# First norm of a two-block layer: its factors moved behind the transposes, a small first transfer, products of zeros at the start, and rstd sums on the vector engine

## Chip, cores and metric

The kernel runs on one core of a Trainium2 chip. The metric is the device time of one execution in microseconds (us), as the median of the timed runs. Five engines work side by side: PE (TensorE: products and transposes), DVE (VectorE), ACT (ScalarE), POOL (GpSimd) and SP (SyncE), which here issues the transfers from memory (DMA). Each engine takes its instructions in its own fixed order.

## The reference, cut to what matters

x is 256 tokens of width 1024, all float32. A first block adds a mixer of three branches and a feed-forward with a short convolution; a second block of two layers follows, then a last norm. Every part begins with a norm. Only the beginning matters here:

```python
def rmsnorm(x, g):
    y = x * lax.rsqrt(jnp.mean(x * x, axis=-1, keepdims=True) + EPS)
    return y * g

def first_block(x, ...):
    h = rmsnorm(x, norm_mix_g)
    c_q, c_kv, k_r, u_ssm, x_q, gate_logits = split_combined(h @ w_in)
    y_a = mla_branch(c_q, c_kv, k_r, ...) @ w_o_mla      # latent attention, rotated
    y_b = s5_branch(u_ssm, ...) @ w_o_ssm                # state space
    y_c = cross_branch(x_q, mem, ...) @ w_o_cross        # attention to mem, its norm first
    x = x + (g0 * y_a + g1 * y_b + g2 * y_c) @ w_out     # g0, g1, g2 = sigmoid(gate_logits)
    ...
```

## The kernel before

**Tiles.** The 256 tokens are two tiles of 128, with the tokens on the partitions. Before a product the normed rows are transposed by PE, so that the width lies on the partitions: eight blocks of 128 rows, four to a bank. Every float32 operand of a product is split into a rounded high part and the rest: for weights `wh` on ACT and `wl` on DVE (`raw` is the transfer's tile, 512 KB each), for normed rows `h` on both. Three products (high-high, high-low, low-high) stand for one. PE is thus the engine with the most work by design.

**The first norm** (`norm_T`, L551, and `norm_rows`, L533): per token tile, ACT squares two halves of 512 columns and sums them (`ss`), DVE multiplies by the gain (`xs`), POOL adds the two sums and EPS and takes the power -0.5 (`rs`), DVE scales `xs` by it, PE transposes (`tr`), ACT and DVE split the bank into `h`. The gain is loaded twice 128 x 512, one row to all partitions (`load_gain`). The first product of `w_in` (`pr`, 512 wide, 48 products for both token tiles) gives the query latents `cq` and a part of `ckv`.

**The state-space branch** (`ssm_setup`, `ssm_maps`, `ssm_half`): from small parameters in the tile `par`, ACT takes a sine and a cosine (`psin`, `pcos`), POOL forms powers of the factors (`pwr`) and from them the input factors `bwr`; DVE multiplies them into maps (`pm`, `xB`, `cT`, `x`), PE transposes those (`tr<-par,xB`) and forms `se`; POOL makes the angles' tables `turn`; DVE turns the inputs (`sp`), scans (`sv`) and turns back (`sg`); PE multiplies by `cT` (`yb<-sg,cT`). This runs in two halves. The second half's `yb` must be there before the glu and the last branch can be done. Meanwhile PE fills its time with gate products (`pt`, 256 wide, from `proj_T`).

**What sets the order.** All instructions are recorded with an estimated cost (`Program.add`, `Engine.cost`) and then issued by a list schedule (`forward`, `issue`): on each engine the ready instruction with the earliest latest-start goes next, within the limits of the tile pools (65 slots `w`, 5 `raw`, 8 banks). Transfers of kind "first" go ahead of all others. Any change of a cost, an operand or an engine can therefore move instructions far away, up to the end of the mixer; behind it the order is nearly the same.

[...]

Of the kernel before, what the change touches and what calls it, by code (L numbers as in the profile page):

```python
# [9 lines left out]
F32 = mybir.dt.float32  # L10
F32R = mybir.dt.float32r
# [31 lines left out]
def region(ap):  # L43
    """The partitions and the elements of a row that an access path may touch."""
    (row, parts), *free = ap.ap
    p, f = divmod(ap.offset, row)
    lo = f + sum(min(0, s * (n - 1)) for s, n in free)
    hi = f + sum(max(0, s * (n - 1)) for s, n in free) + 1
    return p, p + parts, lo, hi
# [10 lines left out]
class Op:  # L60
    """An instruction to come: its engine, its call and its estimated time."""
# [7 lines left out]
class Program:  # L69
    """Records instructions with their data's order and issues them by a list schedule.  # L70

    Per engine, the instruction that is ready and comes first by priority goes next, as long
    as the rest of the program can still run in the order of an earlier schedule within the
    tile pools. The priorities are start times of the schedule that runs from the end.
    """

    ENGINES = ("pe", "act", "dve", "pool", "sp")
    # time from the end of an instruction to the start of one on another engine that waits for it
# [19 lines left out]
    def tile(self, t, tags, whole=False):  # L98
        """Makes a tile known: the pools it takes room in, and if any two accesses keep their order."""
        name = t.tensor.name  # L100
        self.tags[name] = tags
        if whole:
            self.whole.add(name)
        return t

    def add(self, eng, call, cost, reads, writes, kind=""):
        op = Op(eng, call, cost, kind)
        # the vector engine's second port to SBUF is Pool's only one
# [35 lines left out]
    def backward(self, order):  # L144
        """Latest start times, from a schedule that runs from the end, later instructions of order first."""
# [42 lines left out]
    def forward(self, prio, base):  # L188
        """A schedule by priority; base is an order that keeps within the pools."""
# [32 lines left out]
        def room(i, full):  # L222
            """The tiles that op i takes into use, or None when there is no room for them."""
# [126 lines left out]
class Engine:  # L350
    """An engine's calls, recorded with their cost."""
# [33 lines left out]
class Ctx:  # L385
    """Pools, constants, and the blocks shared by all layers."""
# [43 lines left out]
    def weights(self, w, n0, n):  # L430
        """w[:, n0:n0+n] as the two float32r parts of a product, per 128-row block a list of (hi, lo)."""
# [34 lines left out]
    def mm3(self, ps, x, w, start, stop):  # L466
        """ps (+)= x.T @ w, the small product of the low parts left to float32's rounding."""
# [4 lines left out]
    def mm_rows(self, ps, xs, ws, start, stop):  # L472
        """ps[i] (+)= sum over k of xs[k].T @ ws[i][k], the products with the low parts of x last."""
# [16 lines left out]
    def rstd(self, ss, n, count):  # L490
        m = self.sm("rs_m", n)
        self.pool.tensor_scalar(out=m, in0=ss, scalar1=1.0 / count, scalar2=EPS, op0=ALU.mult, op1=ALU.add)
# [3 lines left out]

    def split(self, src, hi, lo, scale=None):
        """Splits float32 data into two float32r parts, scaled by a constant or per partition."""
# [14 lines left out]
    def transposes(self, src, name="tr"):  # L513
        """[128, 128 n] to a bank with the n blocks transposed."""
# [11 lines left out]
    def load_gain(self, src, kind="load"):  # L526
        """A gain vector of 1024, on all partitions."""
# [5 lines left out]
    def norm_rows(self, halves, g):  # L533
        """rmsnorm of [128, 1024] rows given as two halves."""
        ss = self.sm("ss", 2)
        xs = [self.w("xs") for _ in range(2)]
        for b in range(2):
            junk = self.w("junk")
            # D is an even power of two: the scale is exact
            self.act.activation(out=junk, in_=halves[b], func=AF.Square, scale=D ** -0.5, accum_out=ss[:, b:b + 1])  # L540
            self.dve.tensor_tensor(out=xs[b], in0=halves[b], in1=g[b], op=ALU.mult)
        s1, r = self.sm("s1", 1), self.sm("rs", 1)
        self.pool.tensor_scalar(out=s1, in0=ss[:, 0:1], scalar1=EPS, scalar2=None, op0=ALU.add)
        self.pool.tensor_tensor(out=s1, in0=s1, in1=ss[:, 1:2], op=ALU.add)
        self.pool.tensor_tensor(out=r, in0=s1, in1=self.mhalf[:, :1], op=ALU.pow)
# [4 lines left out]
    def norm_T(self, tiles, g):  # L550
        """rmsnorm of 256 rows, transposed and split: per half of the width (hi, lo), each [128, 2, 4, 128]."""  # L551
# [9 lines left out]

    def split_tokens(self, ps, dst, t):
        """Splits [128, 4 * 128] into the columns of token tile t of dst."""
# [3 lines left out]
    def norm_x(self, gain):  # L567
        """The norm of both token tiles of x, for the products to come."""
# [10 lines left out]
    def proj(self, w, n0, n, x=None, rows=False):  # L579
        """x.T @ w[:, n0:n0+n], per token tile; with rows one tile after the other."""  # L580
# [19 lines left out]
    def proj_T(self, w, n0, x=None):  # L600
        """w[:, n0:n0+256].T @ x for all tokens: two blocks of 128 rows in a bank."""
# [14 lines left out]
    def merge_out(self, m, scale, w):  # L616
        """x += (scale * m).T @ w, m as four tiles of two 128-row blocks of all tokens."""
# [16 lines left out]
    def swiglu(self, w1, w3, w2):  # L634
        """x += 0.5 * (silu(h w1) * (h w3)) w2."""
# [22 lines left out]
    def conv_swiglu(self, w_up, w_down, cw, cb):  # L658
        """x += (silu(g) * v) w_down with [g | v] the causal convolution of h w_up along the tokens."""
# [39 lines left out]
    def feed_forward(self, w1, w3, w2, gate_rows, gate, scale):  # L699
        """x += scale * gate(h w1, h w3) w2, by chunks of the inner width.  # L700

        The first chunk takes the token tiles one after the other, as the norm hands them over."""
# [43 lines left out]
    def gate_proj(self, w, n0, bias=None):  # L746
        """Gate of one branch, two blocks of 128 rows to a tile; with half the bias, tanh of half the logits."""
# [839 lines left out]
```

## Time and profile before

| | us |
|---|---|
| median of 3 runs (lowest to highest) | 1621.19 (1621.08 to 1621.62) |
| span of the profiled execution, first to last instruction | 1619.3 |
| PE busy in the span | 1589.3 (98%) |
| DVE, ACT, POOL busy | 1019.0, 843.1, 134.9 |

The profiled execution's own time is known by its span only; the median of the timed runs is 1.9 us longer, for what lies around the span. An engine's busy time counts from an instruction's start to its end, so the instructions of one engine may overlap a little. PE's own waits are few and lie nearly all in the first 220 us.

### The profile page before, as it was taken

What the parts mean: (1) busy time and instruction counts of PE and PEld (TensorE: products, weight loads), DVE (VectorE), ACT (ScalarE), POOL (GpSimd) and SP (SyncE); (2) the same over time, 40 slices, a digit from 0 to 9 for tenths busy, and PEclk for the clock granted to TensorE, in tenths of its full rate; (3) what the DMA queues carried; (4) which work ended last, traced back from release to release, by engine and by line L of the source; (5) the groups of instructions that cost most, each with busy time, mean ns of one, the idle gap of its engine ahead of it and who ended that gap; (6) DMA issues with size and microseconds to landing.
All of it is one profiled execution on the core that took longest, in us unless ns stands there. A gap on an engine that the chain in (4) does not pass through costs nothing.

```text
span 1619.3 us, 28502 instructions
## 1 busy us (share of the span) xinstructions
PE 1589.3 (98%) x11126; PEld 1455.3 (90%) x11126; DVE 1019.0 (63%) x1759; ACT 843.1 (52%) x1746; POOL 134.9 (8%) x276
## 2 busy tenths in 40 slices
PE   7999999999999999999999999999999999999998
PEld 6889989899989999889998999899998899989997
DVE  6678797787676545755657554665457556574543
ACT  6984554665555434555446443454345554464431
POOL 4554500000000000000000000000000000000000
PEclk9999999999999999999999999999999999999999
DMA  8731464665557575454647666475654546475650
GB/s 258 232 104 53 148 208 130 221 202 176 184 171 248 170 228 183 145 181 137 195 138 234 195 197 193 142 243 169 224 182 146 180 137 196 137 236 194 197 181 26
DMA packets 214374, 288.30 MB, mean 178 GB/s; under 512 B 13792, under 2 KB 170080, under 8 KB 214240
## 3 DMA queue, kind: packets, MB, share of 16 engines
q1 hardware_dynamic: 214240, 286.49, 55.6%
q8 instruction: 87, 1.43, 0.4%
q14 instruction: 47, 0.39, 0.1%
HBM read 284.88 MB, written 1.05 MB: 177 GB/s over the span
## 4 chain that ended last, share of the span: by engine, by line
PE 91%; DVE 4%; ACT 2%; DMA 2%; issue 1%; POOL 0%; SPq 0%; POOLq 0%; DVEq 0%; ACTq 0%
PE pt L463 50%; PE acc L463 22%; PE pr L463 7%; PE up L463 7%; PE tr L488 2%; DVE wl L379 1%; ACT wh L379 1%; PE yb L463 1%; DMA x<-in_x_dram 0%; DVE sbp L379 0%; DVE pm L379 0%; PE rs L463 0%; DMA raw<-in_w_mem_kv_dram 0%; PE glu L463 0%; ACT sqh L379 0%
## 5 line engine op out<-in xcount | busy, mean ns | idle before, releaser
L379 DVE TENSOR_TENSOR wl<-raw,wh 128x512 fp32r<-128x512 f32 x1045 | 661.3, 685 | 210.3 <-ACT wh L379 189.5
L463 PE MATMUL pt<-h,wh 128*128 128x256 f32 x4224 | 758.4, 282 | 0.1
L379 ACT CAST wh<-raw 128x512 fp32r<-128x512 f32 x1045 | 580.5, 618 | 158.4 <-DMA raw<-in_w_in_dram 48.1
L463 PEld LDWEIGHTS pt<-h,wh 128*128 128x128 f32 x4224 | 650.3, 188 | 3.4 <-ACT gate L379 0.3
L463 PE MATMUL pt<-h,wl 128*128 128x256 f32 x2112 | 593.2, 281 | 0.0
L463 PEld LDWEIGHTS pt<-h,wl 128*128 128x128 f32 x2112 | 397.7, 188 | 0.2 <-issue 0.2
L463 PE MATMUL acc<-wh,gh 128*128 128x512 f32 x440 | 173.7, 395 | 0.0
L463 PE MATMUL acc<-wh,gl 128*128 128x512 f32 x440 | 173.2, 394 | 0.0
L463 PE MATMUL acc<-wl,gh 128*128 128x512 f32 x440 | 173.2, 394 | 0.0
L463 PE MATMUL pr<-wh,h 128*128 128x512 f32 (+2 forms) x480 | 134.6, 362 | 2.1 <-ACT h L379 1.5
L379 ACT CAST gh<-sg 128x512 fp32r<-128x512 f32 x47 | 29.1, 620 | 151.5 <-DVE sg L379 151.5
L463 PE MATMUL up<-wh,h 128*128 128x512 f32 x320 | 102.0, 397 | 0.0
L463 PEld LDWEIGHTS pr<-wh,h 128*128 128x128 f32 x480 | 85.5, 189 | 17.2 <-ACT h L379 1.9
L463 PEld LDWEIGHTS acc<-wh,gl 128*128 128x128 f32 x440 | 82.6, 188 | 19.5
L463 PEld LDWEIGHTS acc<-wl,gh 128*128 128x128 f32 x440 | 82.6, 188 | 18.1
L463 PEld LDWEIGHTS acc<-wh,gh 128*128 128x128 f32 x440 | 82.6, 188 | 18.0
L379 POOL TENSOR_SCALAR s<-ss 128x1 f32<-128x1 f32 x20 | 9.9, 494 | 1059.1 <-ACT junk L379 1059.0
L379 DVE TENSOR_TENSOR sg<-sg,pt 128x512 f32<-128x512 f32 x36 | 24.7, 687 | 114.9 <-PE pt L463 114.9
L379 ACT ACTIVATE sg<-pt 128x512 f32<-128x512 f32 x36 | 21.6, 599 | 135.3 <-PE pt L463 135.3
L463 PE MATMUL pr<-wl,h 128*128 128x512 f32 (+2 forms) x240 | 86.5, 361 | 0.5 <-DVE wl L379 0.5
L463 PEld LDWEIGHTS up<-wh,h 128*128 128x128 f32 x320 | 59.7, 188 | 13.8
L379 ACT ACTIVATE junk<-x 128x512 f32<-128x512 f32 x36 | 22.8, 632 | 87.1 <-DVE x L379 80.9
(346 smaller groups left out, 1665.0 us busy)
## 6 DMA issues: line engine op xcount, KB each, us to landing
raw<-in_w_ffn_dram SPq DMA_DIRECT2D x264, 512.0 KB, 5.0
raw<-in_w_in_dram SPq DMA_DIRECT2D x124, 512.0 KB, 4.9
raw<-in_w_up_dram SPq DMA_DIRECT2D x44, 512.0 KB, 4.9
raw<-in_w_out_dram SPq DMA_DIRECT2D x24, 512.0 KB, 4.1
raw<-in_w_down_dram SPq DMA_DIRECT2D x22, 512.0 KB, 4.4
raw<-in_w_mem_kv_dram SPq DMA_DIRECT2D x8, 512.0 KB, 5.2
raw<-in_w_branch_ret_dram SPq DMA_DIRECT2D x8, 512.0 KB, 3.8
raw<-in_w_o_mla_dram SPq DMA_DIRECT2D x4, 512.0 KB, 4.7
```

Source lines behind the costliest of these rows:

```text
L379: self.prog.add(self.name, lambda: getattr(self.eng, op)(**kw), self.cost(op, kw), list(aps.values()), writes, "fast" if self.name == "dve ...
L463: self.prog.add("pe", lambda: self.nc.tensor.matmul(ps, lhsT=lhsT, rhs=rhs, start=start, stop=stop), ns, [lhsT, rhs], [ps])
L488: self.prog.add("pe", lambda: self.nc.tensor.transpose(out, src, ident), 109, [src, ident], [out])
```

## The change

The first norm alone gets a function of its own, `first_norm`. One square over 1024 columns gives the sum; `xs` is x times rstd, with no gain; after the transposes the width lies on the partitions, so the gain is a column of eight numbers per partition, and the split of each 128-column block takes it as its scale: sixteen small splits on ACT and DVE each instead of four wide ones. The gain and the identity for the transposes form a new tile `par0` (136 columns), loaded behind the first token tile; the other parameters (`par1`, 118 columns) are an ordinary load. `warm_up` adds eleven products of a zeroed tile, 512 columns wide in bfloat16, ahead of all other work of PE; nothing reads their bank. In all norms the sum with EPS moves from POOL to DVE (`row_rstd`, `rstd`), the power stays on POOL. The diff also drops comments and docstrings (left out here).

```diff
     def rstd(self, ss, n, count):
         m = self.sm("rs_m", n)
-        self.pool.tensor_scalar(out=m, in0=ss, scalar1=1.0 / count, scalar2=EPS, op0=ALU.mult, op1=ALU.add)
+        self.dve.tensor_scalar(out=m, in0=ss, scalar1=1.0 / count, scalar2=EPS, op0=ALU.mult, op1=ALU.add)
...
+    def row_rstd(self, ss):
+        s1, r = self.sm("s1", 1), self.sm("rs", 1)
+        if size(ss) == 1:
+            self.dve.tensor_scalar(out=s1, in0=ss, scalar1=EPS, scalar2=None, op0=ALU.add)
+        else:
+            self.dve.tensor_scalar(out=s1, in0=ss[:, 0:1], scalar1=ss[:, 1:2], scalar2=EPS, op0=ALU.add, op1=ALU.add)
+        self.pool.tensor_tensor(out=r, in0=s1, in1=self.mhalf[:, :1], op=ALU.pow)
+        return r
...
     def norm_rows(self, halves, g):
...
-        s1, r = self.sm("s1", 1), self.sm("rs", 1)
-        self.pool.tensor_scalar(out=s1, in0=ss[:, 0:1], scalar1=EPS, scalar2=None, op0=ALU.add)
-        self.pool.tensor_tensor(out=s1, in0=s1, in1=ss[:, 1:2], op=ALU.add)
-        self.pool.tensor_tensor(out=r, in0=s1, in1=self.mhalf[:, :1], op=ALU.pow)
+        r = self.row_rstd(ss)
...
+    def first_norm(self, gcol):
+        out = []
+        for b in range(2):
+            pair = [self.prog.tile(self.hpool.tile([128, 1024], F32R, tag="h", name="h"), ("h",)) for _ in range(2)]
+            out.append([v.rearrange("p (t k c) -> p t k c", t=2, k=4) for v in pair])
+        for t in range(2):
+            ss = self.sm("ss", 1)
+            junk = self.prog.tile(self.rawp.tile([128, 2 * PIECE], F32, tag="raw", name="sq"), ("raw",))
+            self.act.activation(out=junk, in_=self.x[t], func=AF.Square, scale=D ** -0.5, accum_out=ss)
+            r = self.row_rstd(ss)
+            for b in range(2):
+                xs = self.w("xs")
+                self.dve.tensor_scalar(out=xs, in0=self.x_halves(t)[b], scalar1=r, scalar2=None, op0=ALU.mult)
+                ps = self.transposes(xs)
+                for k in range(4):
+                    self.split(ps[:, k * 128:(k + 1) * 128], *(v[:, t, k] for v in out[b]), gcol[:, 4 * b + k:4 * b + k + 1])
+        return out
+
+    def warm_up(self, n):
+        z = self.w("warm", 320).bitcast(BF16)
+        self.dve.memset(z, 0.0)
+        ps = self.bank("warm")
+        for i in range(n):
+            self.prog.add("pe", lambda: self.nc.tensor.matmul(ps, lhsT=z[:, 0:128], rhs=z[:, 128:640], start=True, stop=True),
+                          430.0, [z], [ps], "first")
...
-    PAR1 = (("c_ident", 128), ("ssm_lambda_re", 16), ("ssm_lambda_im", 16), ("ssm_log_dt", 16), ("c_steps", len(STEPS)),
+    PAR0 = (("c_ident", 128), ("norm_mix_g", 8))
+    PAR1 = (("ssm_lambda_re", 16), ("ssm_lambda_im", 16), ("ssm_log_dt", 16), ("c_steps", len(STEPS)),
...
-        par = self.const("par", sum(n for _, n in self.PAR1))
-        self.load(par, a["par1"], "first")
...
+        for key, names, kind in (("par0", self.PAR0, "first"), ("par1", self.PAR1, "load")):
+            par = self.const(key, sum(n for _, n in names))
+            self.load(par, a[key], kind)
...
+        self.warm_up(11)
         self.parameters()
-        g = self.load_gain(a["norm_mix_g"], "first")
         self.load(self.x[1], a["x"][128:256])
-        self.h = self.norm_T([self.x_halves(t) for t in range(2)], g)
+        self.h = self.first_norm(self.par["norm_mix_g"])
...
+    A["norm_mix_g"] = A["norm_mix_g"].reshape(8, 128).T
+    for key, names in (("par0", Ctx.PAR0), ("par1", Ctx.PAR1)):
+        A[key] = np.concatenate([A.pop(n).reshape(128, w) for n, w in names], 1)
```

The change moves instructions on all engines. Three places follow, of before and of the change in turn.

SP's first transfers, of before (`x_79` and `x_80` are the two token tiles, `raw` pieces of `w_in`):

```order
L427 DMA x_79<-in_x_dram 128x512 x2
L427 DMA par<-in_par_dram 128x246
L427 DMA gain<-in_norm_mix_g_dram 128x512 x2
L427 DMA x_80<-in_x_dram 128x1024
L427 DMA raw<-in_w_in_dram 128x2x512 x4
L427 DMA raw<-in_w_in_dram 128x6x160
L427 DMA gq<-in_q_a_norm_g_dram 128x384
```

And of the change:

```order
L427 DMA x_79<-in_x_dram 128x512 x2
L427 DMA par_84<-in_par_dram 128x136
L427 DMA x_80<-in_x_dram 128x1024
L427 DMA raw<-in_w_in_dram 128x2x512 x4
L427 DMA gq<-in_q_a_norm_g_dram 128x384
L427 DMA gkv<-in_kv_a_norm_g_dram 128x256
L427 DMA mem<-in_mem_dram 128x512 x3
L427 DMA gain<-in_mem_norm_g_dram 128x512 x2
L427 DMA raw<-in_w_in_dram 128x6x160
L427 DMA mem<-in_mem_dram 128x512
L427 DMA pos<-in_positions_dram 128x2
```

The two gains are gone and the second token tile follows the small tile directly; the fifth piece of `w_in` has moved behind loads for `mem`, and `par1` stands behind `pos`.

ACT around the sine and the cosine of the state space, of before (`p` are softmax exponentials of the attention, `qkT` and `ych` its operands, `gate` a tanh):

```order
L379 ACT_TABLE_LOAD
L379 ACTIVATE psin<-pv 128x320
L379 CAST ych<-co 128x512 x2
L379 ACTIVATE qkT<-qt,gTq 96x512
L379 ACTIVATE pcos<-pk,hpi 128x320
L379 CAST wh<-raw 128x512
L379 ACTIVATE qkT<-qt,gTk 96x512
L379 CAST wh<-raw 128x512
L379 ACTIVATE qkT<-qt,gTq 96x512
L379 ACTIVATE qkT<-qt,gTk 96x512
L379 ACT_TABLE_LOAD
L379 ACTIVATE p,ls<-ms,nb 128x128 x4
```

And of the change:

```order
L379 ACTIVATE p,ls<-ms,nb 128x128 x4
L379 ACT_TABLE_LOAD
L379 ACTIVATE psin<-pv 128x320
L379 ACT_TABLE_LOAD
L379 ACTIVATE p,ls<-ms,nb 128x256 x2
L379 CAST wh<-raw 128x512
L379 ACTIVATE p,ls<-ms,nb 128x256 x2
L379 ACT_TABLE_LOAD
L379 ACTIVATE pcos<-pk,hpi 128x320
L379 CAST wh<-raw 128x512
L379 COPY p_554<-tr 128x512
```

Sine and cosine have moved into the softmax, with a table load at each turn; one more stands ahead of the `gate` that follows. POOL's work on `pwr` and `bwr` comes behind them.

DVE ahead of the second scan, of before (`sp`, `sv`, `sg` of the second half; `gq` and `yp` belong to the first half's output):

```order
L379 TENSOR_TENSOR gq<-yp 128x512
L379 TENSOR_TENSOR wl<-raw,wh 128x512
L379 TENSOR_SCALAR gq<-gq 128x512
L379 TENSOR_TENSOR wl<-raw,wh 128x512 x4
L379 TENSOR_TENSOR gq<-gq,yp 128x512
L379 SCALAR_TENSOR_TENSOR yp<-gq,yp 128x512
L379 TENSOR_TENSOR wl<-raw,wh 128x512 x4
L379 TENSOR_TENSOR sp<-se,turn 128x512 x2
L379 TENSOR_TENSOR wl<-raw,wh 128x512
L379 TENSOR_TENSOR sp<-se,turn 128x512 x2
```

And of the change:

```order
L379 TENSOR_TENSOR gq<-yp 128x512
L379 TENSOR_TENSOR wl<-raw,wh 128x512 x2
L379 TENSOR_SCALAR gq<-gq 128x512
L379 TENSOR_TENSOR gq<-gq,yp 128x512
L379 TENSOR_TENSOR sp<-se,turn 128x512 x2
L379 TENSOR_TENSOR wl<-raw,wh 128x512
L379 TENSOR_TENSOR sp<-se,turn 128x512 x2
```

Fewer `wl` and one `yp` less stand ahead of the second `sp`; they have moved behind the scan.

## Rows read from the trace of the kernel before

**Rows 1.** The page's head and its busy times.

```profile
span 1619.3 us, 28502 instructions
PE 1589.3 (98%) x11126; PEld 1455.3 (90%) x11126; DVE 1019.0 (63%) x1759; ACT 843.1 (52%) x1746; POOL 134.9 (8%) x276
```

**Rows 2.** Waits of PE: us in total, times, longest us.

```profile
PE tr L488 <- DVE xs L379: 10.8, 2, 10.6
...
PE yb L463 <- DVE sg L379: 3.9, 1, 3.9
```

**Rows 3.** The chain in order of time: start us, us, what.

```profile
3.05 7.66 DMA x<-in_x_dram
...
215.66 3.00 DVE sg L379 x5
218.79 0.46 PE yb L463 x16
...
744.63 90.70 PE pt L463 x768
```

**Rows 4.** Stretches: us, busy (instructions) by engine, PEclk, DMA share, GB/s.

```profile
10.59:18.38 7.79, 6.77 (x22) 5.28 (x23) 6.33 (x13) 6.48 (x16) 4.12 (x10) 1.00 1.08 373
18.38:28.31 9.93, 9.93 (x46) 8.09 (x44) 8.39 (x15) 7.45 (x22) 3.23 (x7) 1.00 0.73 228
...
134.64:219.33 84.69, 77.59 (x800) 73.86 (x796) 73.37 (x142) 41.25 (x88) 29.24 (x33) 1.00 0.42 126
...
219.80:223.20 3.40, 3.40 (x109) 3.23 (x99) 3.40 (x8) 0.58 (x1) 0.00 (x0) 0.50 0.58 178
```

**Rows 5.** ACT's instructions at the start: start us, us, what.

```profile
4.33 0.63 ACT L379 ACTIVATE junk<-x 128x512 f32<-128x512 f32 x1
...
25.45 0.27 ACT L379 COPY ckv<-pr 128x128 f32<-128x128 f32 x1
...
28.31 0.48 ACT L379 COPY cq<-pr 128x384 f32<-128x384 f32 x1 [0.51 <-PE pr L463]
```

**Rows 6.** Other engines at the start, in order of time.

```profile
6.63 0.57 POOL L379 TENSOR_TENSOR rs<-s,mhalf 128x1 f32<-128x1 f32 x1
...
9.45 0.69 DVE L379 TENSOR_TENSOR xs<-x,gain 128x512 f32<-128x512 f32 x1 [1.91 <-DMA gain<-in_norm_mix_g_dram]
10.06 0.88 DVE L379 TENSOR_SCALAR xs<-xs,rs 128x512 f32<-128x512 f32 x2
...
10.59 1.97 PE L488 MATMUL tr<-par,xs 128*128 128x128 f32 x8 [10.59 <-DVE xs L379]
...
13.12 0.79 PE L463 MATMUL pr<-wh,h 128*128 128x512 f32 x1 [0.55 <-ACT wh L379]
...
26.04 0.39 PE L463 MATMUL pr<-wl,h 128*128 128x512 f32 x1
```

**Rows 7.** ACT at the last softmax of the mixer.

```profile
126.16 1.28 ACT L379 ACT_TABLE_LOAD   x1 [2.54 <-PE ms L463]
127.45 0.37 ACT L379 ACTIVATE p<-ms,nb 128x128 f32<-128x128 f32 x1
```

**Rows 8.** POOL in the state-space stretch.

```profile
120.28 0.35 POOL L379 TENSOR_TENSOR pwr<-pcos,mag 128x64 f32<-128x64 f32 x1 [4.11 <-ACT pcos L379]
...
129.37 0.69 POOL L379 TENSOR_TENSOR bwr<-bwr,twr 128x80 f32<-128x80 f32 x1
...
167.86 3.04 POOL L379 TENSOR_TENSOR turn<-pcos 128x512 f32<-128x512 f32 x1 [19.79 <-PE pt L463]
```

**Rows 9.** DVE's groups, 134.6 to 219.4: busy us, mean ns, idle before.

```profile
L379 DVE TENSOR_TENSOR wl<-raw,wh 128x512 fp32r<-128x512 f32 x39 | 25.6, 709 | 0.1
L379 DVE TENSOR_TENSOR cT<-pm 64x256 f32<-64x256 f32 x16 | 6.7, 420 | 0.3
...
L379 DVE TENSOR_TENSOR sp<-se,turn 128x512 f32<-128x512 f32 x8 | 5.2, 683 | 5.5 <-POOL turn L379 5.0 <-PE yb L463 0.5
```

**Rows 10.** PE at the first transposes of the maps.

```profile
138.34 0.60 PE L488 MATMUL tr<-par,xB 128*128 128x128 f32 x4
```

More of the change, by code (lines that the diff above doesn't have):

```diff
@@ L1219, in parameters @@
         a = self.a
-        par = self.const("par", sum(n for _, n in self.PAR1))
-        self.load(par, a["par1"], "first")
-        self.par, o = {}, 0
-        for name, n in self.PAR1:
-            self.par[name] = par[:, o:o + n]
-            o += n
+        self.par = {}
+        for key, names, kind in (("par0", self.PAR0, "first"), ("par1", self.PAR1, "load")):
+            par = self.const(key, sum(n for _, n in names))
+            self.load(par, a[key], kind)
+            o = 0
+            for name, n in names:
+                self.par[name] = par[:, o:o + n]
+                o += n
         self.ident = self.par["c_ident"]
@@ L1567, in lay_out @@
     A.update(shape_constants())
-    A["par1"] = np.concatenate([A.pop(n).reshape(128, w) for n, w in Ctx.PAR1], 1)
+    A["norm_mix_g"] = A["norm_mix_g"].reshape(8, 128).T
+    for key, names in (("par0", Ctx.PAR0), ("par1", Ctx.PAR1)):
+        A[key] = np.concatenate([A.pop(n).reshape(128, w) for n, w in names], 1)
     A["ssm_bc"] = np.concatenate([A.pop(n) for n in ("ssm_b_re", "ssm_b_im", "ssm_c_re", "ssm_c_im")], 1)
```

## The prediction, made before the changed kernel was run

> **What bounds the kernel now.** Start with the page: PE is busy 98% of the span, 1589.3 of 1619.3 us [rows 1]. So only what PE waits for can be won back, plus what it does at its lower clock. The waits of PE [rows 2] name two places: 10.6 us before the first transpose, for `xs` of the vector engine (DVE), and 3.9 us in the state-space stretch, for DVE's `sg`. The chain of waits [rows 3] shows them in order: the transfer of the second token tile of x ends at 10.71; much later DVE's `sg` ends at 218.66, and PE goes on with `yb` at 218.79. From there to the end PE has practically no gaps, so a gain must have arrived by about 220 us.
>
> Last, the stretches [rows 4]. In 10.59 to 18.38 PE does 22 instructions in 7.79 us, in the next 9.93 us 46. [...] (The clock column prints 1.00 for the early stretch; there the durations tell it.) After the 3.9 us wait the column does show the lower level: 0.50 in 219.80 to 223.20.
>
> **The head.** Before, the first tile's norm ends late because `xs = x * gain` waits for the gains, the second half until 9.45; rstd had been ready since 7.20 (6.63 + 0.57) [rows 6]. The change removes these two broadcasts (256 KB each) and four products of 0.69 on DVE.
>
> New first tile. The one square over 1024 columns needs both halves, here by 4.33; two squares of 512 take 0.63 each [rows 5], so it ends by 5.6 with its read. The sum moves from POOL to DVE, 0.1 to 0.2; pow 0.57; the first `xs` 0.44 (0.88 for two [rows 6]): transposes at about 7.0 instead of 10.59, 3.6 us earlier.
>
> Second tile. It lands at 10.71 as the last of 512 + 123 + 512 + 512 KB; now 512 + 68 + 512 KB. The first 512 KB are in by 4.33; the other 580 at 373 GB/s (10.59 to 18.38 [rows 4]) would end at 5.9. From above, the 567 KB less at that rate only bring 10.71 down to 9.2. I take 6.5, near the first: the parameters and gains, 635 KB, went on until 9.45 [rows 6], far under that rate, and the tile of x itself came 1.3 behind them. Square, sum, pow and two `xs` (1.2 + 0.2 + 0.6 + 1.0) free DVE at about 9.5.
>
> Then DVE bounds: `row_rstd` and `xs` of the second tile stand before every splitting. It must make eight `wl` (0.71 [rows 9], 5.7 us) and sixteen low parts of 128 columns. No such row exists on DVE: a quarter of a 512-column split is 0.17, ACT's 128-column copy 0.27 [rows 5]; I take the latter, being of that width: 0.25 to 0.27, 4 us. The last of the eight `wl`, behind four of the small parts, is ready at 16.3; 26 of 48 products are then left, at 0.22 (46 in 9.93 us): 22.0. [...] If the clock drops back in between, up to 2.5 us are lost (22 products at 0.43 instead of 0.22 are 4.6 us, part of it under DVE's work). I take 23.6, against the copy of the second tile's result at 28.31 [rows 5]: the head gives **4.7 us**, between 3 and 6.5. ACT gets sixteen of 0.27 for four full splits (at most 0.63 like its squares), 2 us more, but begins them about 3 us earlier.
>
> The eleven products themselves cost nothing: PE is empty until 7.0, and eleven at 0.43 end near 6. The DVE memset is under 0.44 (a fast 512-column pass), with DVE empty. Without that cover they would cost 4.7. `row_rstd` in the later norms hides under PE's products (rows 2 name no such wait); the last norm has no cover, but there a one-column add on POOL becomes one on DVE, both under the 0.27 of a 128-column copy: nothing, within 0.3 either way. The move of `par1` behind the memory loads matters next.
>
> **The state-space stretch.** The planner reorders all engines up to 220 us. The second ordered piece shows ACT: before, sine and cosine (`psin`, `pcos`) stand between two table loads ahead of the last softmax; POOL's `pwr`, which waits for `pcos`, begins at 120.28 [rows 8]. Now they stand in its midst, with three table loads of 1.28 and a fourth ahead of the `gate` behind, instead of two. The softmax began at 127.45, after a load at 126.16 [rows 7]. Without that load, and 4.7 earlier, it begins at 121.5; four exponentials of 0.37 are 1.5, three loads 3.8, `psin` and `pcos` 0.5 each (estimates, for 320 columns between the 0.37 and the square's 0.63), four wider exponentials 2.0 and a split 0.6: `pcos` ends at 130.4, ten later than before.
>
> [...] The load takes 1.28 and the exponential starts 0.01 behind it [rows 7]. [...]
>
> From `pwr<-pcos` to the end of `bwr` POOL took 120.28 to 130.06, memsets among it [rows 8]. The new order has eleven memsets and a `turn` product (1.07 to 3.04) in that piece; I keep 10 us: `bwr` is ready at 140.4 (130.4 + 10). Before, DVE took it up at 134.64.
>
> From there to the last `sg` DVE was busy 73.37 of 84.69 us [rows 4]. In the new order eight `wl` (0.709) and eight `cT` (0.420 [rows 9]) stand elsewhere, and two more of about 0.7: 10.4 us less, 63.0. Of its 11.3 us of idle time 5.0 were waits for POOL's `turn` [rows 9], which began only at 167.86 [rows 8]; now POOL has its first-half `turn` products right behind `bwr`, the first one even ahead of it. I take 4 us idle (1 to 9): `sg` ready at 207.4. PE has 578 `pt` products before the second half's `yb<-sg` instead of 627: 49 at 0.118 (90.70 us / 768 [rows 3]), 5.8 us now behind it. Before the first transposes of `xB` it has 65 more, 7.7 us. They began at 138.34 [rows 10], so PE would be there at 138.3 - 4.7 + 7.7 = 141.3, and waits for `xB` until 145.4 (`bwr` + 5; before, the first came 3.7 after DVE had taken up `bwr`, and four groups are needed), 4.1 us; so it reaches the last `yb` at 214.9 - 4.7 - 5.8 + 4.1 = 208.5. The later of the two is 208.5, and 5.8 of work have moved behind: 214.3 against 218.8, **4.5 us earlier**. The lower clock at 219.8 (at most 1.7 us in 3.4) I leave as it is.
>
> Sum: span 1619.3 - 4.5 = 1614.8. The median of the runs, 1621.19, lies 1.9 above the profiled span; with that 1616.7. Of these 0.2% (3.2 us) is about what can be told from no change.
>
> **Rivals.**
> Spent in the stretch: the head comes as forecast, but DVE idles 8 to 9 us again, for ACT's `wh` and `yp`. Then `sg` is ready at 211.9 and the gain is 218.8 - 211.9 - 5.8 = 1.1: 1620.1. For it: DVE's idle time had several causes, and only `turn` is planned away. Against: `turn` was half of it.
>
> Slower: POOL runs in order, and `turn` now stands ahead of `fre`, `fim` and `bwr`. Before, POOL stood 19.79 us in front of a `turn` until PE was done with a `pt` [rows 8], harmlessly, since `bwr` was out. If such a wait returns, `bwr` and with it all `xB` wait too. It decides from `bwr` later than about 149.3, where 149.3 + 63.0 + 4 + 5.8 = 222.1 passes the old 218.8 by 3.3; at 152, 6 us: 1627.
>
> Better: PE and DVE meet without a wait, the 3.9 us and the half-clock stretch go, and the head gives 6: about 8.5 us, 1612.7. Against: `xB` is late by the sum above.
>
> The zeros don't do what they should: PE is again at the lower clock when the products come. The transposes are then 0.25 each (1.97 us for eight [rows 6]) and the products 0.43, and the head gives 2.5 less: 1619.2. For it, what lies between: some 3 us with eight transposes only. [...] Against it, here the clock rose at 18.4 out of a stretch with eight transposes in it.
>
> **Chances.** Forecast 0.45, spent 0.26, better 0.12, zeros 0.06, slower 0.11. Of the forecast's own spread (1613.5 to 1619) 0.40 is below 1617.9; with the better case and the lucky part of the spent one (0.04) faster is 0.56; slower is 0.11; the rest, 0.33, is the same. Range 1612.0 to 1623.0: the better case at its foot, the spent one with `bwr` 3 us late at its top; most of the slower case is left out.
>
> **What would show it.** Transposes near 7.0 and the copy of the second `cq` near 23.6 for the head; products of 0.39 before 12 us for the zeros; `pcos` near 130 and the last `bwr` near 140; the last `sg` near 207 and the second-half `yb` at 208 to 209. It is wrong if `bwr` is past 149, if DVE idles over 8 us between `bwr` and the last `sg`, or if a gap after 225 us grows.

## The result, and the profile after

The changed kernel took 1634.36 us (median of four runs, 1631.69 to 1637.47), the kernel before beside it 1621.4 (1621.08 to 1624.25): ratio 1.0077, 95% interval 1.0059 to 1.0095. It is slower by 13 us; the forecast was 1616.7. Timed again in the last experiment, it gave 1634.15 against 1623.21 (1.0064, 1.0048 to 1.008).

The profiled execution has a span of 1632.6 us. Its page begins so (span; then busy time, share and instructions by engine):

```profile
span 1632.6 us, 28473 instructions
PE 1603.1 (98%) x11137; PEld 1466.3 (90%) x11137; DVE 1026.8 (63%) x1808; ACT 844.4 (52%) x1756; POOL 112.7 (7%) x216
```

Against [rows 1] the span grew by 13.3 and PE's busy time by 13.8: PE did not stand idle for longer in all (29.5 us against 30.0), it was busy for longer. The eleven zeros are 4.9 of that (1.25 to 6.11). The rest shows when PE's clock is read. These stretches of PE alone (start:end, length, busy and instructions, granted clock, DMA share, GB/s) are the ones at the lower level, a granted clock of 0.50, behind the head:

```profile
111.76:115.18 3.42, 3.42 (x18) 0.50 0.00 0
135.66:139.07 3.41, 3.41 (x22) 0.50 0.00 0
152.72:166.38 13.66, 13.66 (x75) 0.50 0.18 48
186.86:190.27 3.41, 2.76 (x14) 0.50 0.59 154
227.82:231.23 3.41, 3.41 (x69) 0.50 0.66 180
```

That is 26.7 us of work at a clock of 0.50, where the kernel before had 3.4 [rows 4]. Half of it at most is lost, by estimate from that clock: 13.3 against 1.7. Measured on the same products at the higher clock (under e7 below) four of the five stretches cost 9.1 us, the long one 4.6 of it; with at most 1.4 for the fourth that is some 8 us more than before. In this execution each stretch follows a wait of PE, and the table of PE's waits (total, times, longest) shows which:

```profile
PE tr L488 <- DVE yt L379: 5.0, 1, 5.0
PE co L463 <- ACT pT L379: 3.1, 1, 3.1
PE mo L463 <- ACT p L379: 3.0, 1, 3.0
PE tr L488 <- DVE xs L379: 2.9, 2, 2.2
PE yb L463 <- DVE sg L379: 2.6, 3, 1.6
PE tr L488 <- DVE xB L379: 2.2, 2, 1.2
```

The 10.6 us for `xs` at the start are gone (2.2 now), and `sg` costs less [rows 2]; in their place stand waits for `pT`, `p`, `xB` and `yt` between 107 and 188 us that the kernel before did not have. The total idle time of PE is unchanged, but it has moved from the head, where the clock was low anyway, into the middle, where the clock fell behind each of these waits here (not in every execution, as e7 shows).

**The head** came as forecast. PE's rows at the start (start, us, what; in brackets the idle time before):

```profile
8.32 1.09 PE L488 MATMUL tr<-par,xs 128*128 128x128 f32 x8 [2.22 <-DVE xs L379]
...
10.03 1.91 PE L488 MATMUL tr<-par,xs 128*128 128x128 f32 x8
11.59 0.78 PE L463 MATMUL pr<-wl,h 128*128 128x512 f32 x1
...
22.29 1.16 PE L463 MATMUL pr<-wh,h 128*128 128x512 f32 x5
```

The last five of the 48 wide products start at 22.29; in the kernel before their row starts at 27.18 and is as long (1.16): 4.9 us. The transposes were late (8.32, not 7.0), since ACT's first table load came to stand behind the wait for x (4.42, 1.28 long). The last `wl` was ready at 16.1 (16.3 forecast), but PE had no wait from 9.44 to 30.5: PE's own work set the end, with the fall of the clock for which the forecast had kept 1.6 us. The zeros failed to prevent it: the granted clock was 1.00 until 9.37 and 0.50 until 12.78. The first eight transposes took 1.09, the next eight 1.91, and products of 0.39 to 0.40 came only from 12.9 on. The copy of the second `cq`, the mark that the prediction named, is at 25.43 and not at 23.6: ACT waited 2.30 for weights ahead of it; PE's next wait, 0.6 us for ACT's `cqh`, comes only at 30.5.

**The middle.** Four places, in order of time. First SP's queue and the ACT split that waits behind it:

```profile
86.73 16.49 SPq L427 DMA_DIRECT2D u<-uT  x24
103.32 0.53 SPq L427 DMA_DIRECT2D raw<-in_w_in_dram  x1
```

```profile
107.61 1.14 ACT L379 CAST wh<-raw 128x512 fp32r<-128x512 f32 x2 [4.97 <-DMA raw<-in_w_in_dram]
```

24 small transfers (16 KB, 0.69 us of issuing each on average) stand in one row; the next weights are issued 16.5 us after the first of them, ACT waits 4.97 for these, and PE 3.1 for the copy `pT` that stands behind on ACT. Before, the same transfers were in groups of 4 to 12 between weight loads.

Second, ACT at the last softmax:

```profile
125.60 1.28 ACT L379 ACT_TABLE_LOAD   x1
126.89 0.47 ACT L379 ACTIVATE psin<-pv 128x320 f32<-128x320 f32 x1
127.38 1.28 ACT L379 ACT_TABLE_LOAD   x1
...
131.15 1.28 ACT L379 ACT_TABLE_LOAD   x1
132.44 0.56 ACT L379 ACTIVATE pcos<-pk,hpi 128x320 f32<-128x320 f32 x1
```

Two loads of 1.28 and a sine lie between the narrow exponentials and the wide ones that PE's `mo` needs: its 3.0 us. Against [rows 7] this was foreseen as a delay of `pcos` (130.4 forecast, 133.0 seen), not as a wait of PE.

Third, POOL from `pcos` to `bwr`, and DVE taking it up:

```profile
133.08 0.34 POOL L379 TENSOR_TENSOR pwr<-pcos,mag 128x64 f32<-128x64 f32 x1 [4.81 <-ACT pcos L379]
...
139.62 0.53 POOL L373 MEMSET cT<- 128x512 f32 x1 [3.93 <-DVE pm L379]
...
143.16 0.53 POOL L379 TENSOR_SCALAR are<-pwr 128x16 f32<-128x16 f32 x1
...
147.31 0.67 POOL L379 TENSOR_TENSOR bwr<-bwr,twr 128x80 f32<-128x80 f32 x2
```

```profile
147.69 1.43 DVE L379 TENSOR_TENSOR pm<-sbc,bwr 128x512 f32<-128x512 f32 x2 [3.33 <-POOL bwr L379]
```

`bwr` is out at 148.0 instead of the forecast 140.4 and the 130.06 of before [rows 8]. The `turn` product ahead of it did no harm (1.06 us, no wait); the memsets did: they stood ahead of `are` on POOL and waited 3.93 us for DVE's `pm` and 1.63 and 0.17 for PE.

Fourth, DVE at 179 to 187 with POOL beside it, and PE's transposes that wait:

```profile
178.78 8.20 DVE L379 TENSOR_TENSOR wl<-raw,wh 128x512 fp32r<-128x512 f32 x7
186.90 0.86 DVE L379 SCALAR_TENSOR_TENSOR yt<-uT,par,yb 128x256 f32<-128x256 f32 x2
```

```profile
178.81 1.58 POOL L379 TENSOR_TENSOR turn<-pcos,psin 128x512 f32<-128x512 f32 x1 [0.85 <-PE pt L463]
180.91 1.57 POOL L379 TENSOR_TENSOR turn<-psin,pcos 128x512 f32<-128x512 f32 x1 [0.51 <-PE yb L463]
182.44 3.39 POOL L379 TENSOR_TENSOR turn<-turn,turn 128x512 f32<-128x512 f32 x2
```

```profile
187.51 0.87 PE L488 MATMUL tr<-par,xB 128*128 128x128 f32 x3 [5.01 <-DVE yt L379]
```

Seven `wl` take 8.20 us, 1.17 each; at 202.5 ten take 6.10, 0.61 each. PE waits for `yt`, which frees the banks, and `yt` stands behind them.

From `bwr` to the last `sg`, DVE's stretch (all engines' busy time) and its largest group read:

```profile
148.44:226.84 78.40, 68.67 (x658) 64.71 (x656) 66.61 (x124) 33.56 (x75) 21.11 (x17) 0.89 0.37 109
```

```profile
L379 DVE TENSOR_TENSOR wl<-raw,wh 128x512 fp32r<-128x512 f32 x31 | 24.3, 844 | 2.4 <-PE kT L463 1.5 <-PE pt L463 0.8
```

They answer to [rows 4, 9]: 66.6 busy and 11.8 idle, where 63.0 and 4 were reckoned.

### The profile page after: what moved, and what is told of

It is laid out like the page before. It is cut to its first block, busy times and chain, and to the rows that moved or that the text cites. A ratio compares the mean times of both kernels' runs of the same rounds, so it can differ in the third digit from the quotient of the medians.

```text
span 1632.6 us, 28473 instructions
## 1 busy us (share of the span) xinstructions
PE 1603.1 (98%) x11137; PEld 1466.3 (90%) x11137; DVE 1026.8 (63%) x1808; ACT 844.4 (52%) x1756; POOL 112.7 (7%) x216
## 4 chain that ended last, share of the span: by engine, by line
PE 90%; DVE 4%; ACT 3%; DMA 2%; issue 1%; POOL 0%; POOLq 0%; DVEq 0%; SPq 0%; ACTq 0%
PE pt L463 49%; PE acc L463 22%; PE pr L463 7%; PE up L463 6%; PE tr L488 2%; DVE wl L379 1%; ACT wh L379 1%; DMA raw<-in_w_ffn_dram 1%; PE se L463 1%; DMA raw<-in_w_in_dram 1%; DVE sbp L379 0%; ACT p L379 0%; DMA raw<-in_w_q_b_dram 0%; PE rs L463 0%; PE glu L463 0%
## 5 line engine op out<-in xcount | busy, mean ns | idle before, releaser
L379 POOL TENSOR_TENSOR rs<-s,mhalf 128x1 f32<-128x1 f32 x20 | 16.6, 829 | 1106.3 <-DVE s L379 1106.3
L463 PE MATMUL up<-wl,h 128*128 128x512 f32 x160 | 63.0, 394 | 0.0
```

The lines of the kernel that those rows point to most:

```text
L379: self.prog.add(self.name, lambda: getattr(self.eng, op)(**kw), self.cost(op, kw), list(aps.values()), writes, "fast" if self.name == "dve ...
L463: self.prog.add("pe", lambda: self.nc.tensor.matmul(ps, lhsT=lhsT, rhs=rhs, start=start, stop=stop), ns, [lhsT, rhs], [ps])
```

## The experiments

Theory 1: the instructions of the change cost nothing; the loss is made by the order that the planner came to for the middle. Rivals: the zeros spend clock that is missed later (2), the sums burden DVE (3), `par1`'s late transfer as such is the cause (4). Times are medians; each ratio is against the kernel before, run beside it.

| run | edit | us | ratio (95% interval) |
|---|---|---|---|
| e1 | changed, no zeros | 1634.09 | 1.0064 (1.0051 to 1.0077) |
| e2 | before, with the sums on DVE | 1619.41 | 0.9979 (0.997 to 0.9987) |
| e3 | changed, `par1` first | 1617.74 | 0.9967 (0.9955 to 0.9979) |
| e4 | changed, old order, first try | 1626.44 | 1.0023 (1.0014 to 1.0033) |
| e5 | changed, old order, head kept | 1621.21 | 0.9988 (0.9978 to 0.9998) |
| e6 | changed, `bwr` early | 1627.97 | 1.0028 (1.0017 to 1.004) |
| e7 | changed, `yt` first | 1631.03 | 1.0045 (1.0031 to 1.0058) |
| e8 | e3, weights ahead of `u` | 1612.67 | 0.994 (0.9925 to 0.9955) |
| e9 | changed, sums on POOL | 1628.94 | 1.0047 (1.0034 to 1.006) |
| e10 | e8, 22 zeros | 1612.27 | 0.9942 (0.993 to 0.9953) |
| e11 | changed, sine beside cosine | 1630.66 | 1.0052 (1.0038 to 1.0066) |
| e12 | e6, e7 and e11 at once | 1629.11 | 1.0049 (1.0036 to 1.0061) |
| e13 | changed, planned in more rounds | 1621.95 | 0.9996 (0.9983 to 1.0008) |
| e14 | `par1` first, sine late, 22 zeros | 1618.56 | 0.997 (0.9959 to 0.9982) |
| e15 | the changed kernel again | 1634.15 | 1.0064 (1.0048 to 1.008) |

**e1, no zeros.**

```diff
-        self.warm_up(11)
```

> The changed kernel without its eleven products of zeros; every other instruction keeps its place on its engine. Theory 1 (the loss is made between 105 and 230 us by the planned order: bwr late, PE waiting, its clock falling behind the waits): that stretch stays as it is, and the head loses what the zeros gave, 0 to 2.5 us: 1634 to 1637 us. Theory 2 (the zeros use up something, and the clock falls later for it): the low-clock stretches of 111 to 190 us go, and the time falls by up to 11 us, to 1623 to 1628.

The time is the changed kernel's. Up to 33 us PE is 1.1 us later, then a wait takes that up. The low-clock stretches stay (133, 150 and 184 us): theory 2 falls, and the eleven zeros are worth nothing here. One difference prices a fall of the clock: the wait at 108 is here too (2.89), but the clock stayed up behind it, and from 116 us on the same products come 1.8 us sooner than in the changed kernel, 0.3 of it from the wait.

**e2, the sums alone.**

```diff
-        self.pool.tensor_scalar(out=m, in0=ss, ...)          # rstd
+        self.dve.tensor_scalar(out=m, in0=ss, ...)
```

(and the one sum of `norm_rows` likewise)

> The kernel before, with only the sums of rstd moved to the vector engine. The planner sets its own order; sine and cosine again stand ahead of the last softmax, with ten table loads. Theory 1: no cost of its own, 1618 to 1624 us, wherever bwr ends before 135 us. Theory 3 (the vector engine, which bounds the state-space stretch, pays for the sums): slower, 1627 to 1634.

Slightly faster than before, in an order of its own; `bwr` ends at 127.3. Theory 3 falls.

**e3, one word, and e8, four loads moved.**

```diff
-("par1", self.PAR1, "load")
+("par1", self.PAR1, "first")
```

> The changed kernel with one word changed: the transfer of par1 is of the kind that goes first. The planner then puts sine and cosine beside those of the rotary tables (eight table loads instead of twelve). Theory 1: pcos ends before 100 us, bwr before 135, the 13.7 us at the lower clock and the waits of 3 us around it go: 1612 to 1620. Theory 3: still slower than the kernel before, 1626 or more.

As theory 1 has it: `pcos` at 80 us, `bwr` at 126.0. One long wait remained ahead of the maps, 3.3 us at 101.5: again 24 `u` transfers ahead of the weights. For e8 each of four weight loads goes to the first place among the `u` at which the five buffers have room:

```diff
-            for i in best[1]:
+            for i in self.hoist(best[1]):
```

> e3 with four weight loads moved up between the 24 small transfers of u that stand before them on the load queue, as far as the five buffers allow; nothing else moves. Theory 1: the wait of 3.3 us at 101.5 us (its weights were issued at 98.28, behind 16.6 us of issuing u) goes, and the half-clock stretch behind it: 3 to 5 us below e3's 1617.7, 1612.5 to 1615. Rival: the stretch at 145 to 175 us waits longer by as much, since the vector engine sets its end: 1616.5 to 1618.

SP's queue of e8:

```profile
83.76 0.54 SPq L447 DMA_DIRECT2D raw<-in_w_in_dram  x1
84.34 4.57 SPq L447 DMA_DIRECT2D u<-uT  x7
89.02 0.53 SPq L447 DMA_DIRECT2D raw<-in_w_in_dram  x1
89.59 6.89 SPq L447 DMA_DIRECT2D u<-uT  x10
```

The wait and the half clock at 105 are gone, and 4 to 5 us with them (by the ratios, by the times): the queue's order alone, no transfer saved.

**e4 and e5, the old order.** The changed kernel's instructions, issued in a fixed order in place of the planner's:

```diff
-            for i in best[1]:
+            for i in order:      # read from a table: the order before, behind the head
```

> The changed kernel's instructions, but from the first wide products on in the order, engine by engine, that they have in the kernel before (the sums of rstd on the vector engine where they stood on POOL); the new head keeps its own order, and par1 is loaded behind the second pair of weights. Theory 1: head gain kept, middle as before: 1614 to 1618 us, bwr about 4 us ahead of the 130.06 of before. Theories 2 and 3: 1626 to 1634, since the zeros and the sums on the vector engine are all there.

e4 did not test it: it also moved `par1` and the first splits about in the head, and PE's wide products ended 3.3 us later than before. From there to 170 us every product kept these 3.1 to 3.3 us, so the middle did replay.

> e4 again, with its head mended: up to the end of the 48 first wide products every engine and the load queue keep the changed kernel's order, word for word; from there on they take the order of the kernel before, engine by engine. Theory 1 (the loss is in the planned order of the middle): PE's lead of 4 to 5 us at 30 us is still there at 200 us, and the end comes 3 to 5 us ahead of the kernel before: ratio 0.997 to 0.998. If the changed instructions themselves cost it (sums on the vector engine, zeros): ratio 1.005 or more.

With the head kept PE is 4.2 to 4.7 us ahead of the kernel before at 27 to 35 us. By 45 us it is 3.2, by 62 us 1.4: a wait of 1.81 at 50.3, which the kernel before has as well (1.55 at 53.5), here with the clock falling behind it. From 66 to 300 us the lead is 0.2 to 2.0, and the time is 1.4 below. So in the order of before the change is worth 1.4 us, less than expected, and the same instructions take 12 to 13 us less than in the changed kernel's own order (by the ratios, by the times). `par1` is issued at 14.84 here and at 14.83 in the changed kernel, so e5 speaks against theory 4 too.

**e6, e7, e11 and e12, single waits.** e6:

```diff
+        late = [i for i in order[at:] if i in self.chain]    # are ... bwr, 13 on POOL
+        order = order[:at] + late + [i for i in order[at:] if i not in self.chain]
```

> The changed kernel, with the 13 small products from are to the last bwr moved on POOL ahead of the memsets and the turn that stand before them; nothing else moves. Theory 1a (bwr on POOL alone is the delay): bwr ready at about 138 instead of 148, the waits for xB at 149 and 151 (1.2 and 0.9 us) go and the 13.7 us at half clock behind them, 5 to 9 us in all: 1625 to 1629. Theory 1b (the vector engine stands right behind it with its cT sums until 144.3, and the later waits stay): 0 to 4 us, 1630 to 1634.

`bwr` was out at 140.4, but DVE took it up only after its `cT` products, as theory 1b had it, at 150.22 (147.69 in the changed kernel; this execution was 3.8 us behind by then, with stretches of 6.8 us instead of 3.4 at half clock at 112 and 136):

```profile
150.22 1.88 DVE L383 TENSOR_TENSOR pm<-sbc,bwr 128x512 f32<-128x512 f32 x3
```

Still some 6 us were won by the times, within 1a's numbers. What won them is not shown: the long stretch at half clock from 152.7 on did not come in the profile, but it is missing in those of e7 and e11 too, which do not move `bwr`. e7 puts five `wl` behind `yt`:

```diff
+        order = [i for i in order[:at] if i not in wl] + wl + order[at:]
```

> The changed kernel, with the two yt sums of the first half ahead of five of the seven wl that stand before them on the vector engine (between 179 and 187 us, each up to 1.75 us long beside POOL's turn instead of 0.69). Theory 1: PE's wait of 5.0 us at 182.5 was for the banks that yt frees; it goes to under 1, with the half clock behind it (186.9 to 190.3): 3 to 6 us, 1628 to 1631. Rival: the wait is for something else (xB, the turn products), and nothing changes: 1632 to 1635.

PE's wait for `yt` went, and the transposes waited 2.8 for ACT's `bT` instead: 3 us won, with an interval that overlaps that of e15. The profiled execution is the fastest of ten (1624.31) and tells more. Up to 177 us PE has the changed kernel's products in its order, and nearly its waits (2.3 for `pT`, 3.0 for the softmax, 1.1 and 0.9 for `xB`), and yet the clock stayed up from 13.56 to 177.40. The products of the first, second, third and fifth stretch at half clock ran so in e7:

```profile
110.48:112.37 1.89, 1.89 (x18) 1.00 0.00 0
132.89:134.81 1.92, 1.92 (x23) 1.00 0.00 0
148.65:157.69 9.04, 7.74 (x76) 1.00 0.10 12
220.77:222.62 1.85, 1.85 (x67) 1.00 0.55 167
```

From the same first to the same last product the changed kernel took 3.35, 3.41, 13.66 and 3.40 us. At 170 us e7 is 8.7 ahead of it at the same product, 0.5 of that from the head. So whether a wait is followed by a fall of the clock differs between executions of one order, and one profile shows one draw: the loss that it shows is not the order's alone. e11 moves `psin`:

```diff
+        late = [i for i in order[:at] if i == sine or i in users]
+        order = [i for i in order[:at] if i not in late] + late + order[at:]
```

> The changed kernel with one move on the scalar engine: psin goes from its place between the exponentials to the place right ahead of pcos (with POOL's three products that need it), so that one table load serves both, ten loads in all instead of twelve. Theory 1: the exponentials end 2 to 3 us sooner, PE's wait of 3.0 us at 131 for the softmax goes, and the half clock at 135.7 to 139.1 with it; part is given back at the waits for xB at 149 and 182: 2 to 5 us, 1628 to 1632. Rival (the waits behind take all of it): 1633 to 1635.

PE's wait for the softmax fell from 3.0 to 2.2 only; the interval overlaps that of e15.

> The changed kernel with the moves of e6 (bwr early), e7 (yt first) and e11 (sine together) at once; the run of 24 small u transfers stays. Theory 1 (these waits and the half clock behind them are the loss of the middle): the 3.0, 2.2 and 5.0 us go; with e6's 5 and e7's 2 to 3 as measured and 2 to 5 for the sine, 8 to 13 us: 1620 to 1625, what stays being the 3.2 us of 108 us with its half clock. Rival (each move only hands the wait on): no more than e6 alone, 1626 to 1629.

Together they won no more than e6 alone: 1.2 us of the softmax's wait is left, but those for `xB` grew to 3.1, 2.9 for `bT` came in place of `yt`, and 17 us at half clock follow at 180 (as they do at 185 in e15's profile, where nothing was moved). The rival's time was right; that a wait removed is handed on to the next one is seen for `yt`, in whose place `bT` came.

**e9, the sums back on POOL.**

```diff
-        self.dve.tensor_scalar(out=m, ...)      # rstd and row_rstd
+        self.pool.tensor_scalar(out=m, ...)
```

> The changed kernel with the third part undone: the sums of rstd are back on POOL (in the first norm too), par1 still comes late. The planner makes its own order: sine and cosine still lie apart, with twelve table loads, but the small u transfers stand in eights between weight loads, and bwr is ahead of the memsets. Theory 1 (late par1 alone does not lose; what counts is whether the order stops PE): no wait near 107, bwr by 135: 1615 to 1624. Rival (par1's lateness is the cause by itself): 1629 to 1636.

The median lies between the two, at the foot of the rival's range. The profile is theory 1's: the new order has `pcos` at 97.4, `bwr` at 127.2, no wait over 2.1 us in the mixer behind the head, and the second half's `yb` at 214.30 (218.79 before). But `par1`, though an ordinary load, was not late here: it is issued at 5.94, so e9 does not test its lateness. PE waits 4.9 us in five pieces for ACT's `h` in later feed-forwards, where neither kernel waits for it. The profiled execution (1624.8) is the fastest of its runs, so where the rest of the 1628.94 lies was not seen.

**e10, zeros enough.** Each of the eleven places issues two products:

```diff
+                                         for _ in range(2)],
```

> e8 with two products of zeros in each of the eleven places, 22 in all; everything else keeps its place. In e8 PE was empty from 6.1 to 8.4 us, and its clock fell at 9.3 for 6.8 us. Theory: the second eleven run at 0.22 each and fill that gap to about 8.4; the clock stays up, and the transposes and first wide products of 8.4 to 16.1 us come sooner: PE's lead at 20 us is 4.5 to 6 instead of 3.0, the time 0.5 to 2.5 us below e8's. Rival (the head is bound by the vector engine and the weights there): no change, within 0.5 us. If they end after 8.5 they delay the transposes: up to 2 us slower.

The heads of e8 (first) and e10, PE alone:

```profile
5.90:9.30 3.40, 1.04 (x9) 1.00 1.03 386
9.30:16.10 6.80, 6.57 (x21) 0.50 1.05 359
```

```profile
5.70:8.40 2.70, 2.66 (x13) 1.00 0.99 361
8.40:16.10 7.70, 6.66 (x31) 1.00 1.02 361
```

Now PE has no gap ahead of the transposes, and the clock stays up to 162.7. The same products come 1.3 us sooner at 19 us, 0.5 at 50, 1.2 at 250. The timed difference (0.4 us) is within the intervals: the trace shows a gain of 1.2, the times can't.

**e13, e14 and e15, the order or `par1`?**

```diff
-    def issue(self, tc, rounds=3):
+    def issue(self, tc, rounds=7):
```

> The changed kernel, with seven rounds of the planner instead of three: not one instruction changes, only their order. Late par1, a run of 17 and one of 10 small u transfers, sine and cosine side by side in the midst of the softmax (ten table loads), bwr behind the memsets. Theory 4 (par1's lateness as such is the cause): as slow as the changed kernel, 1630 to 1636. Theory 1 (the particular order is the cause, and any other order draws anew): off by more than 4 us in either direction, likeliest 1622 to 1630, since the sine no longer costs four loads but the u run and bwr stay.

> e10 (par1 first, 22 zeros), but planned with seven rounds and 0.64 us per transfer issue instead of 0.45, and without the move of the weights by hand: the planner puts sine and cosine at the last softmax again (ten table loads), although par1 is there by 8 us; the u run is broken into 4, 13, 4 and 12. Theory 4 (par1 early is what counts): 1610 to 1616, as e8 and e10. Theory 1 (the order counts): with the sine late again bwr ends about 130 to 140 and the stretch loses 4 to 10 us to e10: 1616 to 1624.

> The changed kernel itself once more, as the measure for the other two on the same chip: 1631 to 1637 us.

e13 has e15's instructions, one for one but for two table loads fewer, with `par1` as late (issued at 14.21), and is 12.2 us faster. PE by stretches of 40 us, e15 and then e13:

```profile
100.00:140.00 40.00, 34.52 (x273) 0.91 0.14 35
140.00:180.00 40.00, 37.70 (x282) 0.83 0.22 67
180.00:220.00 40.00, 34.90 (x354) 0.79 0.45 133
```

```profile
100.00:140.00 40.00, 38.46 (x336) 1.00 0.14 34
140.00:180.00 40.00, 34.10 (x278) 0.90 0.40 119
180.00:220.00 40.00, 39.10 (x529) 0.92 0.39 116
```

234 more instructions are done between 100 and 220 us, and less of the time at half clock. Theory 4 falls as the sole cause. A row of 22 `u` transfers (15.45 us from 87.01) stands in e13 too, and no wait of PE over 0.4 us lies between 92 and 125: what such a row costs depends on the load behind it. e14, with `par1` early but the sine late (`bwr` at 139.1), lost 6 us to e10 (4.6 by the ratios), within theory 1's numbers. Not all of it is the sine's: at 82.3 PE waits 3.45 for ACT's `qkT`, and the clock is low for 6.8 us from 85.5 on, long ahead of the sine at 125. That an early `par1` helps because it lets the planner put the sine early fits e3, and is not shown by e14.

## Why the prediction was wrong

- **The head: right.** 4.7 forecast, 4.9 seen, though the transposes were 1.3 late (the table load behind x, which the sum left out) and the zeros of no use. That the sum still fits is in part luck: it had DVE set the end of the wide products, and PE had no wait for DVE behind the first transposes.
- **The state-space stretch: the step that failed.** "4.5 us earlier" was 7.5 later: the second half's `yb` began at 226.29, not 208.5 (before: 218.79 [rows 3]). The 5.8 us of products moved behind it were sized rightly: 7.5 + 5.8 = 13.3, as much as the span grew. By the terms on DVE: `bwr` 148.0 for 140.4 (+7.6); DVE's work 66.6 for 63.0 (+3.6; the 31 `wl` at 0.844 instead of 0.709 alone are 4.2); DVE's idle time 11.8 for 4 (+7.8). Together 19 us, and 0.4 until the stretch that was read begins (148.44): 207.4 became 226.8. Of the idle time 8.6 us were waits for PE (4.0 of them at 192.97, behind PE's wait for `yt`) and none for `turn`. By the terms on PE: the first transposes of `xB` at 150.55 for 145.4 (+5.1), and from there to `yb` 75.7 us for 63.1. Of these 12.6, 5.2 are waits (8.4 for 3.2), and 7.4 are slower work: 13.66 for 7.74 in the long stretch at half clock, at most 1.4 in the fourth.
- **What the step left out.** It followed DVE and POOL with durations of before and gave PE one wait, 4.1 for `xB`. It did not follow SP's queue, where the 24 transfers stood (e3 against e8: worth 4 to 5 us there), nor the banks that `yt` frees (5.0), it took the cut softmax for a delay of `pcos` only, and it left the lower clock "as it is", one stretch of 3.4, when it forecast new waits of PE itself. In this execution that sentence alone is some 8 us.
- **The rivals.** "Slower" had the right stretch and engine and the wrong mechanism: POOL did stand still ahead of `bwr`, for memsets and not for `turn`, and `bwr` stayed under its 149.3. "Spent in the stretch" had the sign right, DVE idle for over 8 us, but only 2.4 of the 11.8 were for `yp`, none for `wh`. The chance of "slower", 0.11, was too small: it was one mishap at one place, while every engine's order was new over 200 us. "The zeros don't do what they should" was true, and cost nothing that the times show.
- **The cause.** Shown: the order makes 12 to 13 us of difference with the same instructions, by medians (e13, e5 against e15). Shown in part: the `u` row (e3 against e8, not in the changed kernel itself) and the memsets ahead of `bwr` (e6, by the times). Open: how the 13 us divide among the waits, since the single moves do not add up and the clock's falls differ between executions (three stretches in e7's profile, up to 177 us the same order, did not come at all).

The best version is e8, or e10 with its zeros: 0.994, 9.6 to 10 us under the kernel before, from the change itself, `par1` first and four loads moved.

## What to carry to other kernels

Where a scheduler orders the program, an edit at one end is a new order everywhere, and the noise of such orders (12 us here) can exceed the edit's worth (1.4): time the edit with the rest of the order held, and several orders with the edit held. In a new order, look in the order of each engine, and of the load queue too, for a run of cheap items ahead of one that is waited for (here 24 transfers, 16.5 us of issuing, ahead of weights). And price a wait of PE in a dense stretch at its length plus what the clock may lose behind it (here 1.5 us in a stretch of 3.4, 4.6 in one of 13.7). Profile an order more than once before a wait is blamed: here the clock fell behind the same waits in one execution and not in another.

## What the hardware showed

- From 152.72 to 166.38 PE was busy for all of 13.66 us and its granted clock stayed at 0.50. It did 64-column products (`se`), transposes, short `kT` products and, from 162.80 on, products of 256 columns; the clock came back at 166.38. The same products ran at a granted clock of 1.00 throughout in e6, e7 and e11 (9.04 to 9.06 us, 1.2 to 1.3 of them idle), so it was not their kind that kept the clock down; what did is open.
- `wl` on DVE and `turn` on POOL ran side by side at 179 to 186 us: the four `wl` that began while a `turn` ran took 1.55 to 1.75 us, the other three of the row 0.68 to 0.69. From 202.5 on the row of `wl` on DVE was unbroken at 0.61 each, and the `turn` beside it took 4.34 (5.27 before, beside eight `wl` in 4.89 us) against 1.07 for the one at 192.71.
- In e10 the granted clock stayed at 1.00 through eight transposes (8.41, 1.09 us) and a gap of 0.59 behind them; in the changed kernel it fell to 0.50 at 9.37, behind a gap of 2.22 and the same eight. That leaves open whether the gap or the transposes let it fall.
